# A hybrid decoder layer on one Trainium2 core: block sums behind their squares, two engines in emission order at the start, and idle products ahead

## The chip, the cores and the metric

The kernel runs on one core of a Trainium2 chip. A core has engines with instruction queues of their own: TensorE (PE in the profile; PEld is its weight load) multiplies matrices into the banks of PSUM; VectorE (DVE), ScalarE (ACT) and GpSimd (POOL) work element by element; SyncE (SP) only issues transfers here, and ScalarE issues some too. Engines wait for each other through semaphores, and each works its own queue strictly in order. The metric is the time in microseconds on the device. Before the change it is 1483.58 us, the median of three runs (1479.41 to 2008.34).

## What is computed

One layer for 1024 prompt tokens and 32 sample tokens (1056 in all) of 1024 channels, all in fp32:

```
h = rmsnorm(x); p = h @ w_in                       # 40 blocks of 128 output columns
three mixers on parts of p: gated short convolution, windowed attention with sinks, spatial gating
merged = sum_i sigmoid(gates_i) * (y_i @ w_branch_i)
x = x + rmsnorm(merged @ w_out)
up = causal_conv(rmsnorm(x) @ w_up) + b
x = x + rmsnorm((silu(a) * b) @ w_down)
rmsnorm(x) = x * rsqrt(mean(x*x) + eps) * g
```

Attention windows for the sample tokens come from a cache, and the outputs include the new caches: two of them (`wk`, `wv`) are mostly a plain copy of 124 old rows per batch entry from one place in HBM to another, 496 KB each.

## The kernel before, in words

**Layout.** Channels lie on the 128 partitions, tokens on the free axis. x is `M8`, eight blocks k = 0..7 of 128 channels; the tokens are cut into three chunks of 352 columns (chunk 0, 1, 2). An fp32 product is made of three faster ones: each operand is split into a high part (a copy rounded to the type fp32r, made by ScalarE with `copy`) and a low part (the difference, made by VectorE with `sub`), and TensorE adds high times high, high times low and low times high. So one unit, 128 output columns by one chunk with eight blocks of channels, is 24 products of 128x352. The normalised input is `H` (high parts in slots 0..7, low parts in 8..15). Weights come from HBM in pieces of 128x512 (`raw`, `xraw`; 256 KB) and are split in the same way into `wh` and `wl`, or into `Y` where they are kept (`make`, `split`).

**The norms.** For a chunk, ScalarE squares x (`sq`, two blocks at a time), VectorE adds the squares up, TensorE sums over the partitions with a vector of ones (`rstd_of`), VectorE adds eps (`rs`), GpSimd raises to the power -0.5 (`factor_of`), TensorE spreads the result over the partitions by transposes (`spread`), ScalarE copies it from PSUM into `R`, and VectorE scales x by it (`scalar_tensor_tensor` on `M`). With `hold` set, VectorE copies the power's result into `ru` first, and so stands still until GpSimd is through.

**The start.** x of chunk 0 and the weights of the first three gate blocks are loaded on SyncE's queue; the norms of the three chunks are started and ended by `start` and `end`, between the units of `first`. A unit's result goes through a sigmoid on ScalarE (`g`) and out to HBM (`sigd`) on ScalarE's queue. Behind the nine units of the first three gate blocks come the three of gate block 19, and then pairs of blocks by Strassen's scheme (seven products of halves instead of eight), for which `combos` prepares sums and differences of x on VectorE and ScalarE, and additions on `xraw` those of the weights.

**Order.** A scheduler sets the order on ScalarE, VectorE, GpSimd and SyncE by its own estimate of time, except where `tc.manual_schedule` is in force: there an engine follows the order in which the program emits. TensorE is under it throughout; VectorE is from the output projection (`order`, `evac_o`, `chain`) to the first convolution units. `hold` is set over the same stretch. The copies to `wk` and `wv` are written behind a step of the merge (`evac_y`); the scheduler places them on ScalarE's queue at the very start.

**The output projection.** For each chunk, eight units (`evac_o`): ScalarE writes the scaled result to `M8` and squares it, VectorE adds the squares up. While the next chunk's units run, `chain` of the chunk before goes on a step at a time: spread the factor, multiply (`rs`), add x again (`xr`), store `x2d`, square (`acc2`, `sq3`), add, and so to the second norm and the new `H`. The products by `ones` that sum `acc2` stand in TensorE's queue at a fixed place, behind the first half of unit 4 of the next chunk.

Of the kernel before, what the change touches and what calls it, by code (L numbers as in the profile page):

```python
# [17 lines left out]
P = 128  # L18
# [21 lines left out]
def body(tc, i, o):  # L40
# [3 lines left out]
    with top, tc.manual_schedule(engines={mybir.EngineType.PE}):  # L44
# [39 lines left out]
        def cc(c):  # L84
            return slice(c * CW, (c + 1) * CW)
# [191 lines left out]
        def drain(*units):  # L277
            for g in units:
                for _ in g:
                    pass  # L280

# [21 lines left out]
        hold = [False]  # L303
# [29 lines left out]
        nc.scalar.dma_start(cst[:, :NC1], i["cst"][:, :NC1])  # L333
# [47 lines left out]
        def load_x(c, k, n=2):  # L381
            nc.sync.dma_start(M8[:, k : k + n, cc(c)], i["x"][c, :, k : k + n, :])

        load(1)
        load_x(0, 0, 1)
        load_x(0, 1, 1)
        for k in (2, 4, 6):
            load_x(0, k)
# [5 lines left out]
        with ExitStack() as gs:  # L394
# [3 lines left out]
            sg = open_pool(gs, "sg", bufs=1)  # L398

# [7 lines left out]
            def first(c, steps):  # L407
                for u in range(3):
                    unit(8, Hhi, Hlo, evac_gate(16 + u), (c,), pieces=2 * u)
                    steps[u]()  # L410

            def normed(c):
                for k0, n in ((0, 1), (1, 1), (2, 2), (4, 2), (6, 2)) if c == 0 else ((0, 2), (2, 2), (4, 2), (6, 2)):
                    x = M8[:, k0 : k0 + n, cc(c)]
                    for k in range(k0, k0 + n):
                        m = M8[:, k, cc(c)]
                        dve.scalar_tensor_tensor(m, m, g_pre[:, k : k + 1], R[:, cc(c)], ALU.mult, ALU.mult)
                    h, l = H[:, k0 : k0 + n, cc(c)], H[:, 8 + k0 : 8 + k0 + n, cc(c)]
                    copy(h, x)
                    sub(l, x, f32(h))  # L420

            later = {}

            def end(c):
                later[c]()
                normed(c)

            nothing = lambda: None
            with tc.tile_pool(name="su", bufs=1) as su:
                def start(c):  # L430
                    acc = su.tile([P, 2, CW], F32, name="acc", bufs=2)
                    for k in range(0, 8, 2):
                        sq = su.tile([P, 2, CW], F32, name="sq", bufs=2) if k else acc
                        act.activation(sq, M8[:, k : k + 2, cc(c)], AF.Square)
                        if k:
                            tt(acc, acc, sq, ALU.add)
                    later[c] = rstd_of([acc[:, 0, :], acc[:, 1, :]], R[:, cc(c)])
# [9 lines left out]
            first(1, [nothing] * 3)  # L447
            drain(combos(M8, 0))
            first(2, [nothing] * 3)
# [409 lines left out]
        with tc.tile_pool(name="pb", bufs=1) as pb:  # L859
# [8 lines left out]
            def evac_y(b, n):  # L868
                def f(c, ps):
# [5 lines left out]
                    last = tt(m, m, s, ALU.add, pool)  # L875
                    if n == 1 and b == 1 and c == 2:
                        with tc.issue_after(last.ins):
                            nc.scalar.dma_start(o["wk"], i["ck"][:, 4:, :])
                            nc.scalar.dma_start(o["wv"], i["cv"][:, 4:, :])
                    if b == 1:  # L880
                        copy(H[:, n, cc(c)], m)
# [12 lines left out]
        sums = {}  # L894

        def evac_o(n, acc):
            def f(c, ps):
                act.activation(M8[:, n, cc(c)], ps, AF.Identity, scale=g_post[:, n : n + 1])
                if c == 2:
                    if n == 0:  # L900
                        act.activation(acc, ps, AF.Square)
                        return
# [422 lines left out]
```

## Time and profile before

| | us |
|---|---|
| median of the three runs | 1483.58 |
| all runs | 2008.34, 1483.58, 1479.41 |
| the profiled execution | 1479.45 |
| its span, first to last instruction | 1477.7 |
| TensorE busy | 1430.0 (97%) |
| VectorE busy | 903.0 (61%) |
| ScalarE busy | 659.0 (45%) |
| GpSimd busy | 248.4 (17%) |

The span is what the rows further down are counted in; 1.8 us of the profiled time lie around it. Busy shares say which engine has the most work, and the waits say where it stands still: the 47.7 us of the span in which TensorE is not busy are all that a better order alone could take away, apart from stretches at TensorE's lower clock.

### The profile page before, as it was taken

The page shows a single profiled execution, that of the slowest core. Times are in us where ns is not written, and L with a number is a line of the kernel's source. Part 1 is how long each engine was busy: PE and PEld are TensorE (multiplying, and loading weights), DVE is VectorE, ACT ScalarE, POOL GpSimd, SP SyncE. Part 2 cuts the span into 40 slices and gives each one's busy share as a digit, 9 for nine tenths or more (in the row PEclk, how much of TensorE's full clock was granted, in tenths as well). Part 3 has the DMA queues.
Part 4 walks back from the last instruction along what each step waited for, and adds up shares of the span by engine and source line. Part 5 has one row for each costly group of instructions (what it writes and reads, how often), then busy time and mean ns, then how long its engine had stood idle before and what let it go on. Part 6 is the DMA issues. An engine that isn't in the chain of part 4 may idle for free.

```text
span 1477.7 us, 25715 instructions
## 1 busy us (share of the span) xinstructions
PE 1430.0 (97%) x10163; PEld 1419.4 (96%) x10163; DVE 903.0 (61%) x1615; ACT 659.0 (45%) x1347; POOL 248.4 (17%) x319
## 2 busy tenths in 40 slices
PE   4899999999999999999899999999999999999997
PEld 4899999999999989999899999999999999999997
DVE  6844445324777546655578877778777783453546
ACT  5444444435776322244446554455544574121333
POOL 2100000012455215520002212222122110000000
PEclk9999999999999999999999999999999999999999
DMA  6222333211001136643232222221222174231315
GB/s 232 77 90 98 103 109 110 92 48 44 30 23 44 60 107 186 189 140 108 82 110 73 78 75 82 85 87 66 72 84 77 54 259 152 73 109 44 86 38 154
DMA packets 77833, 141.40 MB, mean 96 GB/s; under 512 B 8256, under 2 KB 34816, under 8 KB 77696
## 3 DMA queue, kind: packets, MB, share of 16 engines
q1 hardware_dynamic: 64816, 110.77, 23.7%
q10 hardware_dynamic: 12896, 28.98, 5.2%
q8 instruction: 80, 1.31, 0.4%
q14 instruction: 41, 0.34, 0.1%
HBM read 105.58 MB, written 35.16 MB: 95 GB/s over the span
## 4 chain that ended last, share of the span: by engine, by line
PE 90%; DVE 4%; ACT 2%; issue 2%; POOL 1%; DMA 1%; ACTq 0%; SPq 0%; POOLq 0%; DVEq 0%
PE mm L100 54%; PE wb L100 20%; PE aux L100 13%; DVE M L94 1%; POOL rs L311 1%; PE sp L100 1%; ACT M L700 1%; PE aux L713 1%; DMA M<-in_x 1%; DVE M L694 0%; DMA raw<-in_wu 0%; DVE acc L94 0%; DVE Y L97 0%; ACT Y L91 0%; PE aux L320 0%
## 5 line engine op out<-in xcount | busy, mean ns | idle before, releaser
L100 PE MATMUL mm<-Y,wh 128*128 128x264 f32 (+1 forms) x1824 | 363.8, 295 | 0.0
L100 PE MATMUL mm<-H,wh 128*128 128x352 f32 (+1 forms) x1568 | 354.3, 313 | 1.5 <-DVE Y L97 0.9
L100 PEld LDWEIGHTS mm<-Y,wh 128*128 128x128 f32 x1824 | 292.6, 188 | 0.0
L100 PE MATMUL mm<-Y,wl 128*128 128x264 f32 (+1 forms) x912 | 269.4, 295 | 0.0
L100 PEld LDWEIGHTS mm<-H,wh 128*128 128x128 f32 x1568 | 261.6, 188 | 2.5 <-PE aux L100 1.1
L100 PE MATMUL mm<-H,wl 128*128 128x352 f32 (+1 forms) x784 | 243.7, 311 | 0.0
L100 PEld LDWEIGHTS mm<-Y,wl 128*128 128x128 f32 x912 | 171.8, 188 | 0.0
L100 PE MATMUL wb<-H,wh 128*128 128x264 f32 (+1 forms) x720 | 147.7, 298 | 0.0
L91 ACT ACTIVATE wh<-M 128x512 fp32r<-128x512 f32 x126 | 79.5, 631 | 152.8 <-PE aux L100 65.9
L100 PEld LDWEIGHTS mm<-H,wl 128*128 128x128 f32 x784 | 147.3, 188 | 0.0
L91 ACT ACTIVATE wh<-raw 128x512 fp32r<-128x512 f32 (+1 forms) x98 | 58.3, 594 | 169.2 <-PE mm L100 110.6
L1062 DVE SCALAR_TENSOR_TENSOR cz<-U,cst,cz 128x1072 f32<-128x1072 f32 x88 | 113.8, 1330 | 11.0 <-ACT cz L1060 11.0
L100 PEld LDWEIGHTS wb<-H,wh 128*128 128x128 f32 x720 | 116.4, 188 | 0.0
L100 PE MATMUL mm<-H,Y 128*128 128x352 f32 x624 | 107.2, 331 | 2.6 <-DVE H L97 2.6
L100 PE MATMUL wb<-H,wl 128*128 128x264 f32 (+1 forms) x360 | 107.3, 298 | 0.0
L97 DVE TENSOR_TENSOR wl<-M,wh 128x512 fp32r<-128x512 f32 x126 | 86.5, 686 | 32.8 <-ACT wh L91 32.8
L100 PEld LDWEIGHTS mm<-H,Y 128*128 128x128 f32 x624 | 103.1, 192 | 3.0 <-DVE H L97 3.0
L97 DVE TENSOR_TENSOR wl<-xraw,wh 128x512 fp32r<-128x512 f32 x70 | 48.5, 693 | 90.3 <-ACT wh L91 89.8
L311 POOL TENSOR_TENSOR rs<-rs,nhalf 88x4 f32<-88x4 f32 (+2 forms) x12 | 23.6, 1964 | 392.5 <-DVE rs L310 392.5
L94 DVE TENSOR_TENSOR M<-mm,M 128x352 f32<-128x352 f32 (+3 forms) x79 | 39.5, 506 | 76.2 <-PE mm L100 76.2
L94 DVE TENSOR_TENSOR M<-M 128x512 f32<-128x512 f32 (+1 forms) x88 | 69.5, 790 | 27.1 <-DMA M<-in_wu 26.3
L97 DVE TENSOR_TENSOR wl<-raw,wh 128x512 fp32r<-128x512 f32 (+1 forms) x72 | 53.0, 737 | 51.7 <-ACT wh L91 51.7
(222 smaller groups left out, 2635.8 us busy)
## 6 DMA issues: line engine op xcount, KB each, us to landing
M<-in_wu SPq DMA_DIRECT2D x72, 256.0 KB, 2.6
sig<-sigd SPq DMA_DIRECT2D x72, 176.0 KB, 2.9
y2d<-cz ACTq DMA_DIRECT2D x22, 528.0 KB, 2.8
sigd<-M ACTq DMA_DIRECT2D x40, 264.0 KB, 3.4
xraw<-in_win SPq DMA_DIRECT2D x40, 256.0 KB, 2.7
raw<-in_wd SPq DMA_DIRECT2D x40, 256.0 KB, 2.6
raw<-in_win SPq DMA_DIRECT2D x39, 256.0 KB, 2.6
Y<-y2d SPq DMA_DIRECT2D x14, 528.0 KB, 6.6
```

Source lines behind the costliest of these rows:

```text
L91: act.activation(out, in_, AF.Copy)
L94: return eng.tensor_tensor(out, a, b, op=op)
L97: eng.tensor_tensor(out, a, b, op=ALU.subtract)
L100: pe.matmul(out, lhsT, rhs, start=start, stop=stop, skip_group_check=more)
L311: pool.tensor_tensor(v, v, nhalf[:bs, :nb], op=ALU.pow)
L700: act.activation(s[:, h, :], s[:, h, :], AF.Exp, bias=ng[:, h : h + 1], scale=SCALE, accum_out=l[:, h : h + 1])
L713: pe.transpose(pt[:, h * P : (h + 1) * P], s[:, h, kb * P : (kb + 1) * P], ident)
L1062: dve.scalar_tensor_tensor(z, u[:, s : s + CONV], cwf[:, f, s : s + 1], z, ALU.mult, ALU.add)
```

## The change

At the start, x of chunk 0 is loaded in four transfers over two queues (ScalarE's and SyncE's), ahead of the constants and of the weights. 24 products of the unit matrix, whose result nobody reads, stand first in TensorE's queue. All the squares of a chunk are made before VectorE adds them up. ScalarE and VectorE follow the emission order until `order.close()` behind the second `combos`, and `hold` is set there too. The norm of a chunk is cut into four parts, and emitted so that the next chunk's squares and sums stand between them. In the merge, the copies to `wk` and `wv` are placed behind ScalarE's high part instead of GpSimd's sum. In the output projection, the addition of a square is emitted behind the next evacuation (`late`, `flush`), with one sum of 352 columns for every chunk, and in `chain` behind the next pair's scaling (`add_squares`).

```diff
-        hold = [False]
+        hold = [True]
...
-        nc.scalar.dma_start(cst[:, :NC1], i["cst"][:, :NC1])
...
-        load(1)
-        load_x(0, 0, 1)
-        load_x(0, 1, 1)
-        for k in (2, 4, 6):
-            load_x(0, k)
+        for k in (2, 6):
+            load_x(0, k, nc.scalar)
+        nc.scalar.dma_start(cst[:, :NC1], i["cst"][:, :NC1])
+        load_x(0, 0)
+        load_x(0, 4)
         load(4)
...
+            order = ExitStack()
+            order.enter_context(tc.manual_schedule(engines={mybir.EngineType.DVE, mybir.EngineType.Activation}))
+            warmth = aux()
...
             def normed(c):
+                def scale(p):
+                    for k in (2 * p, 2 * p + 1):
                         m = M8[:, k, cc(c)]
                         dve.scalar_tensor_tensor(m, m, g_pre[:, k : k + 1], R[:, cc(c)], ALU.mult, ALU.mult)
+                def part(p):
...
                     copy(h, x)
+                    if p < 3:
+                        scale(p + 1)
                     sub(l, x, f32(h))
+                scale(0)
+                for p in range(4):
+                    part(p)
+                    yield
...
-                make(2)
-                start(0)
-                end(0)
-                start(1)
+                for q in range(24):
+                    mm(warmth[:, 0:P], ident, ident, True, True)
+                acc0 = add(squares(0))
                 make(4)
-                first(0, [lambda: end(1), lambda: start(2), lambda: end(2)])
+                spread0 = rstd_of(acc0, R[:, cc(0)])
+                acc1 = add(squares(1))
+                spread0()
+                n0, n1, n2 = (normed(c) for c in CHUNKS)
+                next(n0)
+                next(n0)
+                spread1 = rstd_of(acc1, R[:, cc(1)])
+                sq = squares(2)
+                drain(n0)
+                g = first(0, 0)
+                next(g)
+                spread1()
+                drain(g)
+                make(6)
+                next(n1)
+                next(n1)
+                drain(first(0, 1), n1)
+                acc2 = add(sq)
+                drain(first(0, 2), first(1, 0))
+                spread2 = rstd_of(acc2, R[:, cc(2)])
+                make(8)
+                g = first(1, 1)
+                next(g)
+                spread2()
+                drain(g)
+                next(n2)
+                next(n2)
+                drain(first(1, 2), n2)
...
+            order.close()
+            hold[0] = False
...
                     if b == 1:
-                        copy(H[:, n, cc(c)], m)
+                        last = act.activation(H[:, n, cc(c)], m, AF.Copy)
+                        if n == 1 and c == 2:
+                            with tc.issue_after(last.ins):
+                                nc.scalar.dma_start(o["wk"], i["ck"][:, 4:, :])
+                                nc.scalar.dma_start(o["wv"], i["cv"][:, 4:, :])
...
+        def flush():
+            while late:
+                tt(*late.pop())
...
+                sq = pc.tile([P, CW], F32, name="sq", bufs=3)
+                act.activation(sq, ps, AF.Square)
+                flush()
+                late.append((acc, acc, sq, ALU.add))
...
+            def add_squares():
+                for q in range(2):
+                    tt(acc2[:, q, :], acc2[:, q, :], sq[q], ALU.add)
...
+                if n > 2:
+                    add_squares()
                 for q in range(2):
-                    if n == 0:
-                        act.activation(acc2[:, q, :], m[:, q, :], AF.Square)
-                    else:
-                        act.activation(sq[q], m[:, q, :], AF.Square)
-                if n:
-                    for q in range(2):
-                        tt(acc2[:, q, :], acc2[:, q, :], sq[q], ALU.add)
+                    act.activation(sq[q] if n else acc2[:, q, :], m[:, q, :], AF.Square)
                 yield
+            add_squares()
```

What this does to the queues is shown at three places. First ScalarE's queue at the very start, before (`cst` are constants, `warm` a first small copy, `M` is x):

```order
L333 DMA cst<-in_cst 128x80
L91 ACT_TABLE_LOAD
L91 ACTIVATE warm<-nhalf 128x4
L878 DMA out_wk<-in_ck 8x15872
L879 DMA out_wv<-in_cv 8x15872
L91 ACTIVATE Y<-raw 128x512
L434 ACTIVATE acc<-M 128x704
L434 ACTIVATE sq<-M 128x704 x3
```

and now:

```order
L376 DMA M<-in_x 128x2x352
L91 ACT_TABLE_LOAD
L91 ACTIVATE warm<-nhalf 128x4
L376 DMA M<-in_x 128x2x352
L380 DMA cst<-in_cst 128x80
L435 ACTIVATE sq<-M 128x704 x4
L91 ACTIVATE Y<-raw 128x512 x3
L91 ACTIVATE Y<-R 128x512
L435 ACTIVATE sq<-M 128x704 x4
L91 ACTIVATE R<-aux 128x352
```

The two copies to `out_wk` and `out_wv` are gone from the start (they now stand in the merge, behind the high part of its second block), two transfers of x take their place, and all eight squares of the chunks 0 and 1 stand ahead of the first `R`.

VectorE's queue from the first norm on, before (`acc` is the sum of squares, `rs` the norm's factor, `H` the low part):

```order
L310 TENSOR_SCALAR rs<-aux 88x4
L94 TENSOR_TENSOR acc<-acc,sq 128x704 x3
L417 SCALAR_TENSOR_TENSOR M<-M,cst,R 128x352 x8
L94 TENSOR_TENSOR acc<-acc,sq 128x704
L97 TENSOR_TENSOR H<-M,H 128x352 x2
L310 TENSOR_SCALAR rs<-aux 88x4
L97 TENSOR_TENSOR H<-M,H 128x2x352
```

and now:

```order
L305 TENSOR_SCALAR rs<-aux 88x4
L309 COPY ru<-rs 88x4
L94 TENSOR_TENSOR sq<-sq 128x704 x3
L416 SCALAR_TENSOR_TENSOR M<-M,cst,R 128x352 x4
L97 TENSOR_TENSOR H<-M,H 128x2x352
L416 SCALAR_TENSOR_TENSOR M<-M,cst,R 128x352 x2
L97 TENSOR_TENSOR H<-M,H 128x2x352
L305 TENSOR_SCALAR rs<-aux 88x4
L309 COPY ru<-rs 88x4
L416 SCALAR_TENSOR_TENSOR M<-M,cst,R 128x352 x2
L97 TENSOR_TENSOR H<-M,H 128x2x352 x2
```

Behind each `rs` stands the copy to `ru`, which waits for GpSimd's power; the additions of a chunk's squares stand together, and the parts of a norm follow one another without weights between them.

VectorE's queue in the output projection, in the chain of chunk 1, up to the last addition to `acc2` before its sums, before (`R` is chunk 2's sum of squares, `Y` the low parts of the next weights):

```order
L94 TENSOR_TENSOR M_78<-M_78,xr_7288 128x2x352
L94 TENSOR_TENSOR acc2_7599<-acc2_7599,sq3_7597 128x352 x2
L94 TENSOR_TENSOR R_76<-R_76,sq_7719 128x352
L94 TENSOR_TENSOR M_78<-M_78,rs_7598 128x2x352
L94 TENSOR_TENSOR M_78<-M_78,xr_7289 128x2x352
L94 TENSOR_TENSOR acc2_7599<-acc2_7599,sq3_7597 128x352 x2
L97 TENSOR_TENSOR Y_77<-raw_7265,Y_77 128x512
L97 TENSOR_TENSOR Y_77<-raw_7678,Y_77 128x512
L94 TENSOR_TENSOR M_78<-M_78,rs_7598 128x2x352
L94 TENSOR_TENSOR M_78<-M_78,xr_7290 128x2x352
L94 TENSOR_TENSOR acc2_7599<-acc2_7599,sq3_7597 128x352 x2
```

and now:

```order
L94 TENSOR_TENSOR M_78<-M_78,xr_7326 128x2x352
L94 TENSOR_TENSOR R_76<-R_76,sq_7709 128x352
L94 TENSOR_TENSOR M_78<-M_78,rs_7643 128x2x352
L94 TENSOR_TENSOR M_78<-M_78,xr_7327 128x2x352
L94 TENSOR_TENSOR acc2_7644<-acc2_7644,sq3_7642 128x352 x2
L97 TENSOR_TENSOR Y_77<-raw_7302,Y_77 128x512
L97 TENSOR_TENSOR Y_77<-raw_7722,Y_77 128x512
L94 TENSOR_TENSOR M_78<-M_78,rs_7643 128x2x352
L94 TENSOR_TENSOR M_78<-M_78,xr_7328 128x2x352
L94 TENSOR_TENSOR acc2_7644<-acc2_7644,sq3_7642 128x352 x2
L94 TENSOR_TENSOR R_76<-R_76,sq_7761 128x352
L94 TENSOR_TENSOR acc2_7644<-acc2_7644,sq3_7642 128x352 x2
```

Each pair of additions to `acc2` stands one pair's scaling further back, the first of them behind the scaling of the third pair, and one addition to `R` more stands ahead of the last pair.

## Rows read from the trace of the kernel before

**Rows 1.** The page: span, and busy time of each engine.

```profile
span 1477.7 us, 25715 instructions
PE 1430.0 (97%) x10163; PEld 1419.4 (96%) x10163; DVE 903.0 (61%) x1615; ACT 659.0 (45%) x1347; POOL 248.4 (17%) x319
```

**Rows 2.** Windows: busy time per engine (instructions), granted clock, DMA share, GB/s.

```profile
0.00:47.50 47.50, 22.14 (x128) 20.83 (x128) 32.49 (x53) 25.84 (x39) 15.49 (x9) 1.00 0.65 221
14.00:22.00 8.00, 5.24 (x33) 4.89 (x34) 6.68 (x12) 6.40 (x11) 1.66 (x1) 1.00 1.06 396
47.50:51.00 3.50, 3.48 (x14) 3.48 (x15) 2.22 (x5) 1.44 (x2) 0.00 (x0) 0.53 0.00 0
48.00:349.00 301.00, 301.00 (x2276) 301.00 (x2275) 135.87 (x224) 128.13 (x259) 10.18 (x10) 0.99 0.26 85
```

**Rows 3.** Waits of PE over the whole span: us in total, times, longest.

```profile
PE aux L100 <- DVE acc L94: 19.7, 4, 14.5
```

**Rows 4.** Timeline of the start: start us, us, engine, line, operation, [idle before <-releaser].

```profile
1.34 1.26 ACTq L878 DMA_DIRECT2D out_wk<-in_ck  x1
10.06 0.79 ACT L434 ACTIVATE acc<-M 128x704 f32<-128x704 f32 x1 [5.40 <-DMA M<-in_x]
14.50 2.51 PE L100 MATMUL aux<-ones,acc 128*88 128x1 f32 x16 [14.50 <-DVE acc L94]
25.73 6.17 PE L100 MATMUL mm<-H,Y 128*128 128x352 f32 x23 [2.60 <-DVE H L97]
26.25 7.21 POOL L311 TENSOR_TENSOR rs<-rs,nhalf 88x4 f32<-88x4 f32 x1 [7.31 <-DVE rs L310]
37.79 1.34 PE L100 MATMUL aux<-ones,acc 128*88 128x1 f32 x16
39.16 2.75 SPq L135 DMA_DIRECT2D xraw<-in_win  x6
57.23 11.82 PE L100 MATMUL mm<-H,Y 128*128 128x352 f32 x72
```

**Rows 5.** Groups by shape, first 60 us: busy us, mean ns, idle before.

```profile
L417 DVE SCALAR_TENSOR_TENSOR M<-M,cst,R 128x352 f32<-128x352 f32 x24 | 12.2, 580 | 4.5 <-ACT R L91 4.5
L97 DVE TENSOR_TENSOR H<-M,H 128x704 fp32r<-128x704 f32 x11 | 9.5, 884 | 0.4 <-ACT H L91 0.4
L94 DVE TENSOR_TENSOR acc<-acc,sq 128x704 f32<-128x704 f32 x9 | 8.0, 888 | 6.6 <-ACT sq L434 6.2
L97 DVE TENSOR_TENSOR Y<-raw,Y 128x512 fp32r<-128x512 f32 x5 | 3.3, 683 | 0.3 <-ACT Y L91 0.3
L91 ACT ACTIVATE Y<-raw 128x512 fp32r<-128x512 f32 x5 | 3.1, 622 | 1.3 <-DMA raw<-in_win 1.3
L403 ACT ACTIVATE g<-mm 128x352 f32<-128x352 f32 x3 | 1.4, 456 | 0.5 <-PE mm L100 0.5
```

**Rows 6.** DMA issues (640 to 660, then 0 to 60): count, KB, us to landing.

```profile
xr<-in_x SPq DMA_DIRECT2D x4, 352.0 KB, 4.5
xraw<-in_win SPq DMA_DIRECT2D x6, 256.0 KB, 4.7
```

**Rows 7.** Groups by shape, whole span: a plain fp32 product with 128 columns.

```profile
L100 PE MATMUL aux<-M 128*64 128x128 f32 x32 | 4.4, 279 | 0.0
```

**Rows 8.** Timeline behind chunk 1's units of the output projection.

```profile
708.45 1.00 POOL L311 TENSOR_TENSOR rs<-rs,nhalf 88x4 f32<-88x4 f32 x1 [13.94 <-DVE rs L310]
709.48 0.17 DVE L314 COPY ru<-rs 88x4 f32<-88x4 f32 x1 [1.12 <-POOL rs L311]
713.92 0.88 DVE L94 TENSOR_TENSOR M<-M,rs 128x704 f32<-128x704 f32 x1
720.99 0.96 DVE L94 TENSOR_TENSOR acc<-acc,sq 128x352 f32<-128x352 f32 x2 [2.32 <-ACT sq L941]
730.75 2.56 PE L100 MATMUL aux<-ones,acc 128*88 128x1 f32 x16 [4.68 <-DVE acc L94]
```

**Rows 9.** Windows: the stretch behind that wait of PE.

```profile
731.00:737.00 6.00, 6.00 (x29) 6.00 (x29) 2.44 (x7) 1.73 (x3) 1.00 (x1) 0.50 0.29 87
```

More of the change, by code (lines that the diff above doesn't have):

```diff
@@ L275, in combos @@
             part(3, b21)
[L277 to L280, printed above, removed]
         def unit(*args, **kw):
@@ L405, in evac_gate, with first, drain @@
                 return f
[L407 to L410, printed above, removed]
+            def first(c, u):
+                return products(8, Hhi, Hlo, evac_gate(16 + u), (c,), pieces=2 * u)
+            def drain(*units):
+                for g in units:
+                    for _ in g:
+                        pass
             def normed(c):
-                for k0, n in ((0, 1), (1, 1), (2, 2), (4, 2), (6, 2)) if c == 0 else ((0, 2), (2, 2), (4, 2), (6, 2)):
-                    x = M8[:, k0 : k0 + n, cc(c)]
-                    for k in range(k0, k0 + n):
+                def scale(p):
+                    for k in (2 * p, 2 * p + 1):
@@ L420, in normed, with squares @@
                     sub(l, x, f32(h))
[L422 to L428, printed above, removed]
+                scale(0)
+                for p in range(4):
+                    part(p)
+                    yield
             with tc.tile_pool(name="su", bufs=1) as su:
-                def start(c):
-                    acc = su.tile([P, 2, CW], F32, name="acc", bufs=2)
+                def squares(c):
+                    r = []
@@ L444, in body, with add @@
-                first(0, [lambda: end(1), lambda: start(2), lambda: end(2)])
+                        r.append(su.tile([P, 2, CW], F32, name="sq", bufs=8))
+                        act.activation(r[-1], M8[:, k : k + 2, cc(c)], AF.Square)
+                    return r
+                def add(tiles):
+                    for t in tiles[1:]:
+                        tt(tiles[0], tiles[0], t, ALU.add)
+                    return [tiles[0][:, q, :] for q in range(2)]
+                for q in range(24):
+                    mm(warmth[:, 0:P], ident, ident, True, True)
@@ L446, in body @@
             xraw[0] = sx
-            first(1, [nothing] * 3)
             drain(combos(M8, 0))
-            first(2, [nothing] * 3)
+            drain(*(first(2, u) for u in range(3)))
             taken[0] = 6
@@ L874, in f @@
                     tt(s, ps, s, ALU.mult)
[L875 to L879, printed above, removed]
-                    if b == 1:
-                        copy(H[:, n, cc(c)], m)
+                    tt(m, m, s, ALU.add, pool)
+                    if b == 1:
+                        last = act.activation(H[:, n, cc(c)], m, AF.Copy)
[3 more added lines that the diff above has]
+                                nc.scalar.dma_start(o["wv"], i["cv"][:, 4:, :])
                         sub(H[:, 8 + n, cc(c)], m, f32(H[:, n, cc(c)]))
@@ L893, in body @@
         pc = open_pool(pcs, "pc", bufs=1)
-        sums = {}
+        late = []
+        def flush():
+            while late:
+                tt(*late.pop())
         def evac_o(n, acc):
@@ L924, in chain @@
             queue = nc.sync if c < 2 else nc.scalar
+            flush()
             yield
@@ L987, in body @@
                 sq = pair("sq3")
-                steps.append(chain(c, acc, pc.tile([P, CW], F32, name="rs"), xr, pair("acc2"),
+                steps.append(chain(c, [acc], pc.tile([P, CW], F32, name="rs"), xr, pair("acc2"),
                                    [sq[:, 0, :], sq[:, 1, :]], iter(())))
+        flush()
         pcs.close()
```

31 lines of the change are left out of this document (7 added, 24 removed).

## Prediction

> **What bounds the kernel now.** I read the page first: TensorE is busy for 1430.0 of 1477.7 us [rows 1]. Nothing on the other engines is worth anything unless TensorE waits for it or runs at its lower clock because of it. The windows then show where the missing 47.7 us lie: 25.4 of them in the first 47.5 us, and none from 48 to 349 [rows 2]. The list of waits names the heaviest releaser, VectorE's sums of squares, with 19.7 us in four waits [rows 3]: 14.5 at the very start, and 4.68 in the output projection, where the sums of chunk 1's second norm come late [rows 8]. The other idle microseconds (attention, the last norm) are not touched. So there are two places. The reader should follow VectorE in both.
>
> The start, in the timeline [rows 4]: the first square runs at 10.06, after 5.4 us of waiting for x, behind which the copies of `wk` and `wv` were issued at 1.34. The sums begin at 14.50, the first real unit's main stretch at 25.73. A power on GpSimd takes 7.21 us there, while VectorE streams; in the output projection, where VectorE stands still for it, 1.00 [rows 8]. TensorE runs without a gap only from the last spread factor on, and chunk 2's first unit, the second of the three units that start at 57.23, ends at 57.23 + 48 x 0.164 = 65.1 us. I use that as the mark: from there on TensorE has the same work in both kernels.
>
> **The start, reckoned anew.** VectorE and ScalarE now follow the printed order, so I add along it, with durations per instruction from [rows 5]: a scaling 0.51 (12.2 / 24), a low part of H 0.86 (9.5 / 11), an addition of squares 0.89, a 128x512 low part or addition 0.67, a high part of weights 0.62, a sigmoid 0.46.
>
> 1. *x.* The last quarter of chunk 0 takes the place of `wk` on ScalarE's queue, so it is issued by 2.6 (1.34 + 1.26). Four transfers of that size issued together took 4.5 us [rows 6]: 7.1. Its square 0.79 [rows 4], the addition 0.89: the sum is ready at 8.8 instead of 14.5.
> 2. *Idle products.* An fp32 product is two rows (eight sums are sixteen rows), so 24 are 48 rows. One with 128 columns takes 0.137 at the upper clock (4.4 / 32, [rows 7]): 6.6 us, twice that at the lower. They start when the unit matrix is there, which I put at 1.4. The early window prints a granted clock of 1.00, but the sums at 14.5 took 157 ns each and those at 37.8 84 ns [rows 4], so the start runs at 1.2 GHz. After TensorE's two long waits 1.2 GHz held for 3.5 us [rows 2] and about 6 us [rows 9] of work. With 3.5 to 6 low, the products end at 9.7 to 11; I take 10.5. The sums stand behind them: this costs 1.7 us, which VectorE's next work partly hides.
> 3. *Factor.* Sums 1.34, then reading, power and copy 1.4 (1.00 and 0.17 in [rows 8], the rest hand-overs): 13.2. VectorE must now add chunk 1's squares, 2.7, before it scales: 15.9. Those squares need x of chunk 1; 3.9 MB lie up to there at 396 GB/s [rows 2], from about 3 us on, so it lands at 12.9 and its last square is done at 13.7: hidden.
> 4. *Chunk 0.* Eight scalings 4.1, four low parts 3.5, and in between the next factor 1.4: 24.9; six last products, 1.0: the first unit ends at 25.9 (before: 31.9).
> 5. *Chunk 1.* In emission order the third gate block's weights come first: sigmoid 0.46, two high parts 1.25, the last low part 0.67: 28.3. Scalings and low parts 7.6: 35.9.
> 6. *Chunk 2.* Additions 2.7, sums 1.34, factor 1.4: 41.3. Two weight parts 1.3, four scalings 2.0: 44.7. Here VectorE has two additions on `xraw` in its way. Those pieces take the room of the squares, so they can be issued only after the sums, at 39.9; the fourth is issued 1.4 later (2.75 / 6 apart, [rows 4]) and lands 4.7 after that [rows 6]: 46.0. Additions to 47.4, then the rest of the norm 5.5, products 1.0: chunk 2's first unit ends at 53.9.
>
> TensorE itself needs six units of 3.9 and 1.8 for sums and factors after 25.9, so 51.1: it waits 2.8 in all for VectorE, and those 2.8 also hide most of a stretch at the lower clock. For the part that isn't hidden, six products of the first unit at half rate, I subtract 0.8. Gain: 65.1 - 53.9 - 0.8 = **10.4 us**. Bounds: with x 3 us earlier, idle products all at the upper clock and no wait for `xraw`, the scaling starts at 14.6 and 1.3 goes at the end: 13.8. With idle products and sums all at the lower clock (end 14.6, sums 2.5, factor 1.4, additions 2.7) it starts at 21.2: 5.1.
>
> A rule speaks against the idle products. The Trainium skill, TensorE: Matmul & The Clock Gate, Part 1, says that the array starts at half clock, that work releases it, and that an idle stretch throttles it again. Between the sums and the first unit TensorE has only short pieces here, so by that rule the release would be lost before real products come; the rows agree that a long wait brings 1.2 GHz back [rows 2, 9]. What it would do here is a rival below.
>
> **The output projection.** TensorE is ready for chunk 1's second sums at 726.1 and waits until 730.75; the six microseconds behind show a granted clock of 0.50, 1.2 GHz [rows 8, 9], which costs 3.1. So 7.8 us are lost. VectorE's time from 713.92 goes into work and into waits for ScalarE's squares, 2.32 in the first of them [rows 8]; ScalarE in turn waits there for weights. With each addition one scaling further back, VectorE has before the sums: eight multiplications and additions on M at 0.91 (0.88 and the gap), four weight parts at 0.67, six additions to acc2 and two to R at 0.48 (0.96 / 2): 13.8, so 727.7. The last pair of squares has only one addition to R ahead of it and stands behind two weight copies: 0.8 more, 728.5. TensorE still waits 2.4, about as long as the 2.60 in [rows 4], after which products and sums were soon at the upper rate (84 ns at 37.8); so I take the lower clock as avoided. Gain 7.8 - 2.4 = **5.4**. Bounds: 6.4 if only the work counts, 0 if the wait stays long enough for the clock to fall.
>
> **Costs put at nothing.** Chunk 2's chain gains its waits back but shares one buffer of squares, so the last addition moves behind a weight part: 0, give or take 1. `wk` and `wv` now run during the merge beside the loads of sigmoids and weights; these are fetched a whole block of 72 products ahead (11.8 us, the three units in [rows 4]), and at the start the copies held x back by about 3 (10.06 against 7.1), at most by the whole 5.4 that ScalarE waited [rows 4]. So 0; at worst 5.4. ScalarE's `Copy` for `copy` is the same instruction. The early additions in evac_o are as many columns as before.
>
> **Sum.** 10.4 + 5.4 = 15.8 off the profiled execution's 1479.45: **1463.6 us**. That execution is 4.1 under the median of the three runs and 0.04 above the lowest.
>
> **Rivals.**
> - *The second wait stays* (0.17): ScalarE's weight copies still hold the squares, the wait is again near 4.7 us and 1.2 GHz follows: 1479.4 - 10.4 = 1469.
> - *Clock lost at the start* (0.13): between the sums and the first unit TensorE mostly waits, and as behind the waits of [rows 2, 9] the first real units then run some 6 us at 1.2 GHz: 3 us, of which 0.8 is counted: 1466. This is what the rule above comes to.
> - *Idle products too long* (0.08): all at 1.2 GHz, 5.1 + 5.4: 1469.
> - *More* (0.08): both upper bounds, 20.2: 1459.
> - *The copies collide* (0.07): 5.4 back: 1469.
> - *Slower* (0.03): in emission order, high parts of H stand behind a sigmoid that waits for the unit just issued. If that loop closes (sigmoid 0.46, two high parts 1.6, a low part 0.86: 2.9 per unit) it must do so in six of the nine units to eat 15.8; in all nine, 26: 1490. Against it: only four pairs of high parts stand so, and in the sum above VectorE comes later than the sigmoid each time. That the change doesn't do what it says is excluded by the printed queues.
>
> **How the numbers follow.** The forecast has 0.44. Its own range is 1460 to 1467. The range of 1456 to 1473 takes in all rivals but the slower one, and 4 us of spread between executions. About 2% is what a measurement of this kernel can tell from no change, 29.7 us: more than both upper bounds together, so faster by that much has 0.02, slower 0.01, within it 0.97.
>
> **What would show it.** After: the first square near 5 to 7 us and the first sums near 10.5; powers of about 1.0 at the start; the first unit's end near 26, chunk 2's first unit's near 54; TensorE gapless until some 337; and a wait of 2 to 3 us with a granted clock of 1.00 in the second place, near 715. I am wrong if the three first factors wait for something on ScalarE, or if the second wait comes back with 0.50 behind it.

## The result, and the profile after

The changed kernel takes **1466.08 us** in the median of four runs (1468.9, 1467.67, 1464.49, 1462.09), against 1483.59 of the kernel before on the same chip: a ratio of **0.9889, 95% interval 0.9852 to 0.9927**. The ratio is that of the means, without the one slow run of the kernel before (2008.34). That is 1.1% faster, well clear of 1, and 2.5 us above the forecast of 1463.6. The four runs go with their mean granted clock: 0.987, 0.989, 0.991, 0.993, in that order. The profiled one is the slowest of them.

The page of the profiled execution answers to [rows 1]:

```profile
span 1467.1 us, 25813 instructions
PE 1438.9 (98%) x10211; PEld 1428.3 (97%) x10211; DVE 901.2 (61%) x1623; ACT 659.4 (45%) x1346; POOL 235.2 (16%) x319
```

The span is 10.6 us shorter, yet TensorE is busy for 8.9 us more. The idle products are 7.1 of that (and their 48 rows are all that TensorE has more to do); the rest is real work at the lower clock. TensorE now waits for 28.2 us in all, in place of 47.7.

Timeline of the start, for comparison with [rows 4] (start us, us, engine, line, operation, [idle before <-releaser]):

```profile
1.43 7.08 PE L100 MATMUL aux<-ident 128*128 128x128 f32 x48 [1.43 <-POOL ident masks.py:199]
4.64 1.47 ACT L435 ACTIVATE sq<-M 128x704 f32<-128x704 f32 x2 [1.77 <-DMA M<-in_x]
...
8.38 0.17 DVE L820 TENSOR_SCALAR nsink<-cst 128x10 f32<-128x10 f32 x1 [1.35 <-DMA cst<-in_cst]
8.47 1.89 DVE L94 TENSOR_TENSOR sq<-sq 128x704 f32<-128x704 f32 x2
...
10.41 1.71 PE L100 MATMUL aux<-ones,sq 128*88 128x1 f32 x16 [1.89 <-DVE sq L94]
17.06 2.48 PE L100 MATMUL aux<-ones,sq 128*88 128x1 f32 x16 [2.03 <-DVE sq L94]
19.39 3.98 PE L100 MATMUL mm<-H,Y 128*128 128x352 f32 x12
21.64 1.01 POOL L306 TENSOR_TENSOR rs<-rs,nhalf 88x4 f32<-88x4 f32 x1 [7.71 <-DVE rs L305]
24.69 11.47 PE L100 MATMUL mm<-H,Y 128*128 128x352 f32 x59 [0.37 <-DVE H L97]
28.32 0.47 ACT L400 ACTIVATE g<-mm 128x352 f32<-128x352 f32 x1 [2.00 <-PE mm L100]
29.88 1.29 DVE L97 TENSOR_TENSOR Y<-raw,Y 128x512 fp32r<-128x512 f32 x2 [4.29 <-ACT Y L91]
41.30 1.80 PE L100 MATMUL aux<-ones,sq 128*88 128x1 f32 x16 [1.27 <-DVE sq L94]
42.95 3.87 PE L100 MATMUL wb<-H,Y 128*128 128x352 f32 x12
47.94 2.07 DVE L416 SCALAR_TENSOR_TENSOR M<-M,cst,R 128x352 f32<-128x352 f32 x4 [2.17 <-ACT R L91]
66.63 0.48 PE L100 MATMUL wb<-H,wh 128*128 128x352 f32 x2
```

The first square runs at 4.64 instead of 10.06, the first sums at 10.41 instead of 14.50, and GpSimd's power for chunk 1 takes 1.01 instead of 7.21. But twelve products take 3.98 us, 0.33 each, where [rows 4] gives 0.164 (11.82 / 72): that is half rate, and it comes a second time at 42.95. The windows name it (us, busy time of PE, PEld, DVE, ACT, POOL, then the granted clock, DMA share, GB/s):

```profile
12.00:20.00 8.00, 3.90 (x23) 3.49 (x24) 6.66 (x13) 4.47 (x7) 1.01 (x1) 0.50 0.89 329
20.00:28.00 8.00, 7.63 (x28) 7.07 (x28) 4.40 (x9) 5.55 (x8) 1.01 (x1) 0.50 0.01 2
42.00:48.00 6.00, 6.00 (x28) 5.93 (x28) 1.59 (x5) 0.54 (x2) 1.00 (x1) 0.51 0.78 263
722.00:728.00 6.00, 6.00 (x25) 6.00 (x25) 1.32 (x5) 2.06 (x4) 1.00 (x1) 0.50 0.29 90
```

Four stretches, 28 us, stand at 0.50, that is 1.2 GHz. The last lies in the output projection, behind the sums that answer to [rows 8]:

```profile
719.97 0.96 DVE L94 TENSOR_TENSOR acc<-acc,sq 128x352 f32<-128x352 f32 x2 [1.27 <-ACT sq L972]
720.64 2.29 PE L100 MATMUL aux<-ones,acc 128*88 128x1 f32 x16 [1.78 <-DVE acc L94]
```

The wait there is 1.78 us instead of 4.68; the lower clock behind it is the same as in [rows 9].

**Two marks** part the gain in all that follows. A is the first product of gate block 19, right behind the nine units of the start: 72.76 before, 66.63 after. B is the first of the sums named `cz`, behind the output projection: 768.18 and 757.67. Before, A and B, then after, B:

```profile
72.76 0.48 PE L100 MATMUL wb<-H,wh 128*128 128x352 f32 x2
768.18 1.64 PE L100 MATMUL aux<-ones,cz 128*88 128x1 f32 x16 [0.64 <-issue]
```

```profile
757.67 1.34 PE L100 MATMUL aux<-ones,cz 128*88 128x1 f32 x16
```

From B to the end every kernel here takes 709.3 to 709.7 us. So the start gave 6.1, and the stretch from A to B, 695.4 before and 691.0 after, gave 4.4.

### The profile page after: what moved, and what is told of

It reads as the page before. It is cut to its first block, busy times and chain, and to the rows that moved or that the text cites. A ratio compares the mean times of both kernels' runs of the same rounds, so it can differ in the third digit from the quotient of the medians.

```text
span 1467.1 us, 25813 instructions
## 1 busy us (share of the span) xinstructions
PE 1438.9 (98%) x10211; PEld 1428.3 (97%) x10211; DVE 901.2 (61%) x1623; ACT 659.4 (45%) x1346; POOL 235.2 (16%) x319
## 4 chain that ended last, share of the span: by engine, by line
PE 91%; DVE 4%; ACT 2%; issue 2%; DMA 1%; SPq 0%; POOL 0%; ACTq 0%; POOLq 0%; DVEq 0%
PE mm L100 55%; PE wb L100 21%; PE aux L100 13%; DVE M L94 1%; PE sp L100 1%; ACT M L731 1%; PE aux L744 1%; DVE Y L97 1%; DVE M L416 1%; DVE M L725 0%; DMA M<-in_x 0%; DVE H L97 0%; DMA cst<-in_cst 0%; DVE M L604 0%; ACT Y L91 0%
## 5 line engine op out<-in xcount | busy, mean ns | idle before, releaser
L91 ACT ACTIVATE U<-mm 128x264 f32<-128x264 f32 (+4 forms) x199 | 63.8, 342 | 44.9 <-PE mm L100 42.5
```

The lines of the kernel that those rows point to most:

```text
L91: act.activation(out, in_, AF.Copy)
```

## The experiments

My theory: the change's steps do what was reckoned, and what the first profile lacks of the reckoned 15.8 us (it has 10.5) is TensorE's lower clock. The rivals: VectorE's chain is longer than reckoned; the copies to `wk` and `wv` or the idle products are priced wrongly. Each kernel ran beside the kernel before. One profile each gives the marks.

| kernel | median us (runs) | ratio to before, 95% interval | mark A | A to B |
|---|---|---|---|---|
| before | 1483.59 | 1 | 72.76 | 695.4 |
| after | 1466.08 (4) | 0.9889, 0.9852 to 0.9927 | 66.63 | 691.0 |
| the same again, e11 | 1465.42 (6) | 0.9896, 0.9873 to 0.9919 | 62.46 | 689.4 |
| e2 no idle products | 1467.58 (5) | 0.9905, 0.989 to 0.9921 | 65.66 | 689.9 |
| e3 copies first | 1471.34 (6) | 0.993, 0.9915 to 0.9945 | 68.59 | 690.8 |
| e4 no hold | 1465.71 (6) | 0.989, 0.9869 to 0.9911 | 63.20 | 692.5 |
| e5 old projection | 1468.89 (6) | 0.9918, 0.9902 to 0.9934 | 62.25 | 694.6 |
| e9 projection alone | 1476.26 (12) | 0.996, 0.9947 to 0.9972 | 74.17 | 690.3 |
| e6 early weights | 1466.17 (6) | 0.9889, 0.9868 to 0.991 | 60.73 | 692.3 |
| e1 idle products at the start | 1462.42 (4) | 0.987, 0.9853 to 0.9887 | 62.46 | 688.0 |
| e7 idle products in the projection | 1462.70 (6) | 0.9875, 0.9854 to 0.9896 | 62.35 | 687.9 |
| e10 both | 1462.66 (4) | 0.9874, 0.9855 to 0.9893 | 62.32 | 688.8 |
| e8 both, and early weights | 1462.18 (6) | 0.9872, 0.9849 to 0.9895 | 61.95 | 687.8 |
| e12 e1, constants on GpSimd | 1463.73 (4) | 0.9869, 0.985 to 0.9887 | 61.78 | 688.2 |

**The same kernel again (e11).** No edit.

> The changed kernel once more, unaltered, beside the other two. Theory: its time depends on where the clock's level falls at the start and in the projection in the execution at hand: median 1463 to 1467, runs spread over some 5 us, slower than the version with idle products in both places by 2 to 4 us. Rival: the spread lies between chips and not between executions: all its runs within 1 us, and the other version no faster.

Its runs are 1461.6, 1463.04, 1463.09 and then 1467.75, 1468.16, 1469.28; the four of the changed kernel above fall into the same two groups, so five of ten lie at 1461.6 to 1464.5 and five at 1467.7 to 1469.3. The mean clock is 0.991 to 0.994 in the lower group and 0.987 to 0.989 in the upper. Here the profiled run is one of the lower group (1463.04). Its timeline of TensorE:

```profile
10.87 1.41 PE L100 MATMUL aux<-ones,sq 128*88 128x1 f32 x16 [1.55 <-DVE sq L94]
...
17.52 2.48 PE L100 MATMUL aux<-ones,sq 128*88 128x1 f32 x16 [2.03 <-DVE sq L94]
19.86 3.79 PE L100 MATMUL mm<-H,Y 128*128 128x352 f32 x12
...
25.15 9.82 PE L100 MATMUL mm<-H,Y 128*128 128x352 f32 x59 [1.00 <-DVE H L97]
...
40.21 1.38 PE L100 MATMUL aux<-ones,sq 128*88 128x1 f32 x16 [1.37 <-DVE sq L94]
41.45 2.18 PE L100 MATMUL wb<-H,Y 128*128 128x352 f32 x12
...
52.80 5.93 PE L100 MATMUL mm<-H,Y 128*128 128x352 f32 x35 [0.50 <-DVE H L97]
...
62.46 0.48 PE L100 MATMUL wb<-H,wh 128*128 128x352 f32 x2
...
716.45 1.60 PE L100 MATMUL aux<-ones,acc 128*88 128x1 f32 x16 [1.67 <-DVE acc L94]
...
733.38 0.76 PE L100 MATMUL aux<-ones,R 128*88 128x1 f32 x8 [1.30 <-DVE R L94]
```

and its windows:

```profile
20.00:28.00 8.00, 7.00 (x35) 6.48 (x35) 4.86 (x10) 6.47 (x10) 1.01 (x1) 0.79 0.01 3
42.00:48.00 6.00, 6.00 (x41) 5.98 (x40) 4.84 (x10) 2.11 (x4) 0.87 (x1) 1.00 0.97 327
716.00:726.00 10.00, 9.50 (x68) 9.42 (x69) 4.65 (x12) 3.04 (x7) 1.00 (x1) 1.00 0.18 54
```

With the same instructions and almost the same waits, the 59 products take 9.82 instead of 11.47, and the twelve in front of chunk 2's spread factors 2.18 instead of 3.87. Mark A comes 4.2 us earlier. That is more than the 3.3 us of those two rows: the first unit's sigmoid, the weights behind it and so chunk 1's chain come later with it (VectorE's wait of 4.29 above is 2.75 here). The start then gave 10.3, against 10.4 forecast. In the projection the wait is about as long as in the first profile (1.67), but the clock stays, and the stretch A to B gains 6.0 instead of 4.4. That is not the whole 3.0 of a kept clock (half of six microseconds), since the next sums (733.38) wait 1.30 for VectorE. This wait isn't the kept clock's doing: in e1 and e12 below the clock stays too, the wait is missing, and A to B is 688.0 and 688.2. In e11 a weight copy that waited 1.41 us for its load stood ahead of the factor in ScalarE's queue. The rival (spread between chips) is excluded, since both groups occur on one chip. What cost each of the unprofiled runs its time isn't shown: there is one profile of either group.

**No idle products (e2).**

```diff
-                for q in range(24):
-                    mm(warmth[:, 0:P], ident, ident, True, True)
```

> The changed kernel without the 24 idle products. Theory (clock): they end at 8.5 us, two before the sums, and the granted clock falls at 11.7, before the first real product, so they are worth nothing: within 1 us of the changed kernel, ratio near 0.989. Rival (they help): the first sums run at half rate and the first units stay at it longer, 2 to 4 us slower than the changed kernel, ratio 0.991. Rival (they hold the sums back): faster by 1 us or more.

All five runs lie at 1466.8 to 1468.5, close to the upper group of the changed kernel, and none in the lower.

```profile
10.69 2.51 PE L100 MATMUL aux<-ones,sq 128*88 128x1 f32 x16 [10.69 <-DVE sq L94]
...
25.27 11.70 PE L100 MATMUL mm<-H,Y 128*128 128x352 f32 x59 [0.36 <-DVE H L97]
```

The sums take 157 ns each, as those at 14.50 in [rows 4], and the first unit runs at half rate. So the idle products don't shorten a wait. What they do seems to be this: they raise how often the upper level is back early. Seven profiles here have these 24 products and no others at the start. In six of them (e3 to e7 and e11) the 59 products take 9.80 to 9.82 us, in the first profile 11.47, and here 11.70. Between the medians that is 1.5 us, and the intervals overlap.

**Idle products in the waits of the start (e1).** `spin(n)` makes n more of them.

```diff
-                for q in range(24):
+                for q in range(30):
...
                 spread0 = rstd_of(acc0, R[:, cc(0)])
+                spin(8)
...
                 spread0()
+                spin(8)
...
+                spin(2)
                 sq = squares(2)
...
                 spread1()
+                spin(4)
...
+                spin(5)
                 spread2 = rstd_of(acc2, R[:, cc(2)])
```

> The changed kernel with idle products in TensorE's waits of the start too: 30 instead of 24 at first, then 8, 8, 2, 4 and 5 at the five places where TensorE waited for sums and factors. Theory (clock): in the changed kernel the first units ran at 1.2 GHz, and TensorE's products at half rate stand ahead of the spread factors, which is why the start gained 6.1 us instead of 10.4. Then this is 3 to 5 us faster than the changed kernel (ratio to before near 0.986), the window 10 to 48 us prints a granted clock near 1.00, and unit block 19 starts near 62 to 63 us instead of 66.6. Rival (VectorE's chain sets the start, the clock is hidden by it): within 1 us of the changed kernel. Rival (idle products only stand in the way): 1 to 3 us slower than it.

```profile
12.00:20.00 8.00, 6.63 (x61) 6.07 (x60) 6.66 (x13) 4.24 (x6) 1.01 (x1) 0.98 0.96 337
20.00:24.00 4.00, 3.78 (x17) 3.52 (x18) 2.87 (x8) 3.59 (x6) 1.01 (x1) 0.61 0.02 9
24.00:48.00 24.00, 23.62 (x160) 23.20 (x160) 18.03 (x30) 11.63 (x19) 1.01 (x1) 1.00 0.42 138
```

The stretch from 12 to 20, at 0.50 in the changed kernel, is at 0.98, and from 24 on nothing is lost. All four runs lie within 0.8 us of each other (1461.98 to 1462.78), where the ten of the changed kernel spread over 7.7. So small a spread is in part luck: e8, e10 and e12 below have these products too, and the 18 runs of the four versions lie at 1460.9 to 1465.3. But none of the 18 is as slow as the upper group, in which five of ten of the changed kernel lie. (The intervals of the two ratios overlap, so it is these counts that tell them apart.) Behind chunk 2's sums (39 to 51 us) the level was lost in four of the eight profiles with the new start and no such products (the first one, e2, e3, e4), and in none of the four with them. Mark A is no earlier than in e11: the filled waits add no gain to a good execution, they make it the rule.

**Copies first (e3).** The copies to `wk` and `wv` go back to the start, between the two x transfers of ScalarE's queue.

```diff
         load_x(0, 2, nc.scalar)
+        nc.scalar.dma_start(o["wk"], i["ck"][:, 4:, :])
+        nc.scalar.dma_start(o["wv"], i["cv"][:, 4:, :])
         load_x(0, 6, nc.scalar)
```

> The changed kernel with the two copies to wk and wv on ScalarE's queue between the two transfers of x at the start, as they stood before, instead of in the merge. Theory: they held x back by 3 us and more (first square at 10.06 before, 4.64 after), and the rest of the start follows x: 3 to 5 us slower than the changed kernel, ratio near 0.992, last square of chunk 0 at 11 us or later. Rival (the start is set by VectorE's order and x is early enough anyway): within 1 us of it.

```profile
15.16 2.51 PE L100 MATMUL aux<-ones,sq 128*88 128x1 f32 x16 [5.99 <-DVE sq L94]
```

The sums come at 15.16 instead of 10.41 to 10.87, and the median is 5.3 us above the changed kernel's. At this place the copies cost all that x's early landing had won (14.50 before). Mark A still comes 4.2 us earlier than before. The emission order, the norm in four parts, the two queues for x and the idle products share this; the first three were not tried apart. In the merge, between 570 and 660 us, TensorE is busy without a gap beside them in the changed kernel.

**No hold (e4).** `hold = [True]` becomes `[False]`.

> Only the marks that keep GpSimd's powers and VectorE's streaming passes apart at the start are taken out; the rest is the changed kernel. Theory of the prediction: the marks are what shortens the powers from 6.17 and 7.21 us to about 1.0 us; without them at least one of the first three powers lies under VectorE's streaming again and takes 6 to 7 us, and the start loses most of 5 us: ratio to the changed kernel 1.002 to 1.006 (1467 to 1473 us). Rival: the powers stay short because chunk 0's power is issued before VectorE streams, and nothing is lost (within 1 us). Second rival: VectorE, which no longer waits for the powers, starts its passes earlier and a microsecond or two is gained.

The first rival was right about the time. Powers on GpSimd, and VectorE beside them:

```profile
13.49 1.01 POOL L306 TENSOR_TENSOR rs<-rs,nhalf 88x4 f32<-88x4 f32 x1 [12.12 <-DVE rs L305]
13.55 0.89 DVE L94 TENSOR_TENSOR sq<-sq 128x704 f32<-128x704 f32 x1
...
40.56 1.29 DVE L97 TENSOR_TENSOR wl<-raw,wh 128x512 fp32r<-128x512 f32 x2
40.72 1.40 POOL L306 TENSOR_TENSOR rs<-rs,nhalf 88x4 f32<-88x4 f32 x1 [18.09 <-DVE rs L305]
```

Without the marks the powers take 1.01, 1.29 and 1.40 us; the kernel before has 1.66, 7.21 and 5.92 (the 6.17 of the expectation is TensorE's row at 25.73 in [rows 4]). In each case here VectorE runs out of work within 1.3 us and waits for ScalarE or for a load, and the power ends within 0.4 us of that. The one of 7.21 us in [rows 4] covered nine instructions of VectorE without a pause and ended 0.9 us behind the last. So in these traces a power lasts until VectorE's next pause. The rival's reason doesn't hold for the third power, which VectorE's pass at 40.56 covers: the emission order brings the pauses by itself, and the marks add nothing that the runs show. The second rival stays open. Chunk 2's sums begin at 38.85, 1.4 us earlier than in e11, but the twelve products behind them ran at the lower clock (3.53 us), and mark A is at 63.20.

**The two parts apart (e5, e9).** e5 is the changed kernel with the old order of the output projection, e9 the kernel before with the new one. The edit of e5, cut (e9 is its reverse):

```diff
-                flush()
-                late.append((acc, acc, sq, ALU.add))
+                    tt(acc, acc, sq, ALU.add)
...
-                if n > 2:
-                    add_squares()
...
+                if n:
+                    for q in range(2):
+                        tt(acc2[:, q, :], acc2[:, q, :], sq[q], ALU.add)
```

> The changed kernel with the output projection of before: sums by pairs of columns blocks, each addition right behind its square. Theory: the new order there took the wait for chunk 1's second sums from 4.7 to 1.8 us, but in the profiled execution 1.2 GHz followed all the same, so it is worth 3 us, up to 6 in executions where the clock stays up: this is 3 to 5 us slower than the changed kernel, ratio 0.991 to 0.992, with a wait of 4 to 5 us there. Rival (the wait is set by ScalarE's weight copies and moves with them): within 1 us.

> The kernel before with the new order of the output projection and nothing else of the change. Theory: the two parts add up, so this one gives what is left of the whole when the start is taken away. By the marks between the start of attention and the sums that follow the projection it is 4.3 us where the clock falls behind the wait for the second sums and 7.3 us where it does not: 1476 to 1479 (ratio 0.995 to 0.997). Rival: the projection gains only because the earlier start shifts its loads; alone it gives less than 2 us (ratio above 0.9985).

```profile
719.35 2.56 PE L100 MATMUL aux<-ones,acc 128*88 128x1 f32 x16 [3.94 <-DVE acc L94]
```

```profile
728.96 1.60 PE L100 MATMUL aux<-ones,acc 128*88 128x1 f32 x16 [2.43 <-DVE acc L94]
```

The first row is e5's: the old order waits 3.94 us, and A to B stays at 694.6. The second is e9's: 2.43, and A to B falls to 690.3, alone as with the rest of the change. By their ratios both theories held. (e9's mark A, 74.17, also shows by how much the start of the kernel before differs from one execution to another: 1.4 us.) By the ratios e9 gives 0.4% (5.9 us), e5 0.82% (12.2 us); the whole has 1.1% (16.5 us). The parts add up to 18.1, a little more than the whole, within the intervals.

**Early weights (e6).** `make(6)`, which makes ScalarE's high parts of the third gate block, moves from behind `drain(g)` to before `g = first(0, 0)`.

> One statement is moved: ScalarE's high parts of the third gate block's weights are made before chunk 0's first gate block is started, so they no longer stand behind that block's sigmoid. Theory: VectorE's wait of 4.29 us for them at the start goes, its subtractions and chunk 1's chain come 2 to 4 us earlier, and the time falls by 2 to 4 us (1461 to 1463). Rival: at the start TensorE, at half rate, is what is waited for, so VectorE's earlier work only waits elsewhere: within 1 us of the changed kernel. Second rival: the high parts delay ScalarE's part of the first H parts and the first unit, 1 to 2 us slower.

```profile
25.82 1.29 DVE L97 TENSOR_TENSOR Y<-raw,Y 128x512 fp32r<-128x512 f32 x2
```

VectorE's wait of 4.29 is gone, and mark A comes at 60.73, the earliest of all. The time didn't move. In the profiled execution A to B is 692.3: the clock fell behind the wait in the projection, and once more between 400 and 450 (0.97 over these 50 us). Whether the 1.6 us at mark A are a gain stays open; the six runs don't show it.

**Idle products in the projection (e7), in both places (e10), and with the early weights (e8).**

```diff
             yield from wait(3)
+            if c == 1:
+                spin(6)
```

> Six idle products of the unit matrix are put ahead of chunk 1's second block sums in the output projection, in the place of the 1.78 us wait that is left there. Theory: the clock fell to 0.50 in 722 to 728 us because of that wait; with products in it the level stays at 1.00 through 715 to 730 and 2 to 4 us are gained. Rival: the level falls for another reason (the narrow sums and transposes around it) and nothing changes, or the products' own 0.9 us come on top: 0 to 1 us slower.

> The changed kernel with idle products in TensorE's waits of the start and in the projection's wait; the third gate block's high parts stay where they are. Theory: what is left to gain over the changed kernel is the lower clock at these two places, so in an execution where the clock keeps its level in both already there is nothing more to have: time near the fastest runs of the changed kernel, 1460 to 1462 (ratio 0.985 to 0.988), with little spread. Rival: the idle products cost TensorE time of their own that the clock does not give back: 1464 or more.

> The three additions together: idle products in TensorE's waits of the start, the third gate block's high parts made early, and idle products in the projection's wait. Theory: the gains are in different places and add up: 2 to 3 us of the start's idle products (measured alone), 2 to 4 of the early weights if those pay, 2 to 4 of the projection's: 1455 to 1459 us. Rival: with the clock kept, the weights are no longer late, and only the start's and the projection's gains add: 1459 to 1461. Second rival: idle products and early high parts get in each other's way on TensorE, and the sum is no better than the start's alone, 1462.

In e7:

```profile
714.41 1.50 PE L100 MATMUL aux<-ident 128*128 128x128 f32 x12
716.19 1.60 PE L100 MATMUL aux<-ones,acc 128*88 128x1 f32 x16 [0.28 <-DVE acc L94]
```

The clock is 1.00 from 716 to 726 in all three, and A to B falls to 687.8 to 688.8. e10's runs lie within 1.2 us. But e1, e7, e8 and e10 can't be told apart: their medians are 1462.2 to 1462.7. e8's expectation of 1455 to 1459 was wrong: these edits don't add gains, each takes away a loss that a good execution hasn't got.

**Constants on GpSimd (e12).** VectorE's second addition of squares stands behind `nsink`, which waits 1.35 us for constants (8.38 in the timeline above). e12 is e1 with `nsink` on GpSimd, and with 26 idle products at first instead of 30. Of the edit:

```diff
-            dve.tensor_scalar_mul(nsink, sinks, -1.0)
+            pool.tensor_scalar_mul(nsink, sinks, -1.0)
```

> The version with idle products at the start, with one more edit: a small operation on the constants (nsink), which stands in VectorE's queue between the first additions of squares and waits 1.35 us for the constants to land, is given to GpSimd; and 26 idle products stand first in place of 30, so that they end before the sum is ready. Theory: the sum of chunk 0's squares is ready 0.9 us earlier (9.4 in place of 10.3), and as VectorE is what the whole start is reckoned along, the mark behind chunk 2's units comes 0.5 to 1 us earlier and the time falls by as much: 1461.4 to 1462.0, about 0.0005 of the ratio, which timing can hardly tell; the marks can. Rival: VectorE then waits for the same length behind chunk 1's squares, whose x lands when it does, and the mark stays where it is.

```profile
9.60 1.41 PE L100 MATMUL aux<-ones,sq 128*88 128x1 f32 x16
```

The sums come 1.3 us earlier than in e1 (10.87, where they waited for VectorE and not for the idle products), mark A 0.7. The runs (1461.49 to 1465.33) can't show so little.

## Why the prediction was right, point by point

- **Steps 1 and 2, x and the idle products: the sum right, the terms not.** The first sums came at 10.41 and 10.87, reckoned 10.5. But the sum of squares was ready at 10.36, not 8.8, for the most part since two additions stood behind `nsink` (9.54 in e12, without it); and the idle products ended at 8.51 and 9.33, not 10.5. That the two errors cancel is luck. The price of 0.137 us was the wrong one: see the last section.
- **Step 3, the factor.** Powers of 1.01 us as reckoned, though not for the reason given: the order, not the wait on `ru`, makes them short (e4).
- **Steps 4 to 6, the three chunks: right in the execution at the better level.** There chunk 2's first unit ends at 54.6 (52.80 and eleven products of 0.164), reckoned 53.9 and 0.8 for the clock. Here too the sum is better than its terms. In e11 chunk 0's low parts end at 26.05 (reckoned 24.9) and chunk 1's at 37.40 (35.9), but the wait of 1.3 us for `xraw` isn't there: its additions follow the four scalings at once, at 46.57 (46.0). In the first profile the unit ends at 58.8.
- **The failing term is the 0.8 us for the lower clock.** I let it cover six products of the first unit, hidden otherwise by 2.8 us of waits. In the first profile the level was back only at 28 us and was lost again at 42, so that products at half rate stood in front of chunk 2's spread factors and pushed VectorE's chain: 4.9 us instead of 0.8. The rival "clock lost at the start" (0.13, 1466) was this mechanism. Its number met the median, but by luck: its 3 us are too few for the first profile and too many for e11.
- **The rule of the Trainium skill** (TensorE: Matmul & The Clock Gate, Part 1) is that the array starts at half clock, that work releases it and that an idle stretch throttles it again. The traces agree with its first half: e2's first sums take 157 ns each, and the twelve products of its first unit 4.05 us, half rate; and the idle products get faster while they run (last section). With its second half they agree in direction only. In the changed kernel the level fell behind the waits of the start (0.50 from 12 to 20). But it fell in e1 too (0.61 from 20 to 24), where no wait of TensorE between 11 and 24 us is over 0.56 us.
- **The projection.** The wait was reckoned at 2.4 and is 1.67 to 1.78. "I take the lower clock as avoided" held in e11 (gain 6.0 against 5.4) and failed in the first profile (4.4), which showed what the prediction had named as a sign of being wrong, 0.50 behind this wait. Of the nine profiles with the new order and no idle products there, the clock stayed at 1.00 in three.
- **The costs put at nothing** were nothing: the copies in the merge, and chunk 2's chain (from A to B no loss shows beyond the clock and the 1.30 us in e11).
- **Sum.** 10.3 and 6.0 make 16.3 in e11, reckoned 15.8; 6.1 and 4.4 make 10.5 in the first profile. The forecast of 1463.6 lies in the lower group of runs, the median between the groups. Run against run, the means differ by 16.4 us (1482.2 and 1465.8), so the gain is what I reckoned, and the 2.5 us by which the median misses the forecast are about what the execution of 1479.45, from which I subtracted, lies under the mean of its kernel (2.7). That is luck in part: the kernel before varies as well, from 1475.7 to 1485.4 beside the experiments, and I allowed for that in the range, not in the forecast.

## What to carry to other kernels

Where TensorE works in short pieces between waits, a time isn't one number: take several runs with their granted clock before a few microseconds are put down to an edit, and compare marks inside the trace, not ends. Look too at where in its kernel's spread the execution lies from which a forecast is subtracted. Idle products in the waits of the start are worth having for their steadiness (18 runs within 4.4 us, where the changed kernel's ten spread over 7.7) more than for the best time. A GpSimd instruction that is slow beside a busy VectorE, as the power is here, wants a pause of VectorE, and order alone may bring it.

## What the runs showed that I had not expected

**At the start, the column of the granted clock says 1.00 while TensorE runs slowly.** The idle products are 48 rows, two to a product. First a window of the changed kernel (us, busy time of PE, PEld, DVE, ACT, POOL, then the granted clock, DMA share, GB/s), then stretches of the timeline that each hold one rate, two of the changed kernel and one of e6, in which the same products stand first:

```profile
3.40:4.40 1.00, 1.00 (x7) 1.00 (x7) 0.00 (x0) 0.00 (x0) 0.00 (x0) 1.00 1.05 383
```

```profile
1.80 2.77 PE L100 MATMUL aux<-ident 128*128 128x128 f32 x12
...
4.67 3.85 PE L100 MATMUL aux<-ident 128*128 128x128 f32 x33
```

```profile
1.80 5.33 PE L100 MATMUL aux<-ident 128*128 128x128 f32 x24
```

Twelve rows take 2.77 us, 0.23 each, while the column says 1.00; then 33 take 3.85, 0.117 each. From start to start it is 0.213 us and then 0.112, so the 0.137 that I took from [rows 7] for the upper clock lies between the two. The rise came in the fifth microsecond in the changed kernel, in the seventh in e11 and in the eighth in e6, though all three begin at 1.43 with the same products. So 24 products take 7.08, 7.90 or 8.33 us. Before the first fall of the level, durations tell the rate, not that column.

**The length of a wait doesn't tell whether the level falls.** In the projection, waits of 1.47, 1.61, 1.64 and 1.78 us (e6, e4, e3, the changed kernel) were followed by a mean of 0.62 over the nine microseconds from the sums on; waits of 1.67, 1.69 and 1.79 (e11, e12, e1) by 1.00; and waits of 1.98 and 2.43 (e2, e9) by 0.81. What else decides, no run here shows.
